# Group norms centred and spread by fp32r products, and FFN tiles begun earlier, in a decoder block on one core

## The chip, the core and the metric

The kernel runs on one core of one Trainium2 chip. A core has a matrix engine (PE, or TensorE), a vector engine (DVE), a scalar engine (ACT), a general engine (POOL, or GpSimd) and a queue engine (SP) that issues the transfers here. Each works through its own list of instructions in order, and waits on semaphores for the others. The metric is the device time of one execution in microseconds (us).

## The reference

Input is one sequence of 1024 tokens by 1024 channels, all float32. Cut to what matters:

```
h   = modulate(rmsnorm(x), shift1, scale1)
u, v, val, gate = split(h @ w_in + b_in)                     # 512 channels each
y_a = gelu(u) * (causal 128x128 mix of layernorm(gelu(v)) + b_s)
y   = val * sigmoid(gate)
y   = causal depthwise conv of y, width 31, + bias
y_b = silu(layernorm of y over groups of 64 channels)        # the group norm
x   = x + gate1 * (concat(rmsnorm(y_a), rmsnorm(y_b)) @ w_out)
h2  = modulate(rmsnorm(x), shift2, scale2)
x   = x + gate2 * ((silu(h2 @ w_g) * (h2 @ w_up)) @ w_ffn_out)   # FFN width 2816
out = modulate(rmsnorm(x), shift_f, scale_f)
```

## The kernel before

Channels lie on the 128 partitions, tokens along the free dimension, in two halves of 512 tokens. A tile of 128 channels by 512 tokens fits one PSUM bank.

**Products.** A float32 product is made of three fp32r products: each operand is split into a rounded part ("hi", an ACT copy) and the remainder ("lo", a subtraction on DVE or POOL), and PE adds hi x hi, lo x hi and hi x lo in one bank (`mm3`, L680, and `product`, L1068). Small products are left in true fp32, which PE runs as two records each in the trace. The FFN's products use a scheme of seven half-size products (m1 to m7) for eight; the sums of quadrants that this needs are DVE and POOL work (L1175 to L1180 for weights, L1200 to L1214 for activations).

**Stages.** For half 0 and half 1: first norm, projections (u, v, value/gate), spatial mixing, convolution, group norm, `w_out`, second norm. Then the FFN with 22 tiles of its width, its down projection in three rounds, and the last norm, which is written out in three pieces: half 0, then two of 256 tokens.

**Convolution and group norm.** Half 0's taps are shared by DVE and POOL, half 1's are all DVE's (L1006, two tiles at a time in a pair). `group_norm` (L1021) centres each tile by an fp32 product with the matrix `gcen` (L1026), squares on ACT, sums the squares by small products (L1033), takes root and reciprocal (L1036, L1037) and spreads the reciprocals back over channels and tokens: for half 0 by 16 fp32 products of 64 rows and 128 columns per pair (L1046), for half 1 by a block diagonal that DVE writes (`diagonal`, L614) and one fp32r product per tile (L1042).

**Work begun ahead.** For 20 of the 22 FFN tiles the two quadrant products that need only half 0 (m1 and m2, in 24 matmuls of 512 columns) are done by `ahead_quad` (L1082, traced under L1073 with the bank `ah`), and stored in HBM. 12 of them (`N_AHEAD`) are written in the program before half 1's convolution and output projection, 8 (`N_FILL`) behind the second norm of half 1. Each loads a weight tile of 512 KB, has its hi part made by ACT and its lo part (`wl_a`) by POOL, adds once on DVE (L1090) and stores 2 x 256 KB. The two other tiles (20 and 21) are done whole, tile 20 first.

**What sets the order.** The program's text gives only the dependences. `fix_order` (L499) runs a planner forward and backward over all instructions with a table of costs per kind of instruction, and the best of a few such plans becomes the fixed order of each engine. An instruction that the plan puts ahead of another on the same engine holds it up if its operands come late.

**Memory.** Tiles named `s` share four buffers (`tag="s"`, `bufs=4`); the FFN's own tiles take over the memory of the first stages and can be written only when these are through.

## Time and profile before

| | us |
|---|---|
| median of 3 runs | 967.76 (966.22 to 967.87) |
| the profiled execution | 967.97 |
| its span in the profile | 965.9 |
| PE busy / DVE busy / ACT busy / POOL busy | 950.5 / 871.7 / 474.0 / 408.6 |
| granted PE clock, mean | 0.995 |

The profiled execution agrees with the runs. PE's busy time is the union of its instructions, whose ends are modelled, so a PE that is always "busy" can still issue faster or slower: the spacing of its instructions tells which. A matmul's own duration in a row (0.39 us for 512 columns) overlaps the next one. Rows of instructions in order of time give the start, the duration, the engine, line and operation, the output, an arrow and the inputs, and how many alike follow each other; the chain of waits gives start, length and what ran.

### The profile page before, as it was taken

Reading aid. Unit: us, or ns where it says so; the run is one execution under the profiler, and the core shown is the slowest. Engines: PE = TensorE matmul, PEld = TensorE weight load, DVE = VectorE, ACT = ScalarE, POOL = GpSimd, SP = SyncE. Lnnn points to the kernel's source line nnn. Section 1 sums busy time; section 2 is a strip of 40 time slices with the busy share of each in tenths; the row PEclk is TensorE's granted clock in tenths of the full one; section 3 lists DMA queues with packets and bytes.
Section 4 is the critical chain, followed back from the end, with each engine's and each line's share of the span. In section 5 each row is a group of like instructions: output and inputs, shape, how many; then the busy total and the mean of one; then the engine's idle time right before and its main releaser. Section 6 shows DMA issues by size and latency. Waiting matters only on the chain.

```text
span 965.9 us, 12960 instructions
## 1 busy us (share of the span) xinstructions
PE 950.5 (98%) x4521; PEld 769.6 (80%) x4521; DVE 871.7 (90%) x1236; ACT 474.0 (49%) x756; POOL 408.6 (42%) x241
## 2 busy tenths in 40 slices
PE   8999999999999999999999999999999999999996
PEld 4887777778777778788888888888888888888885
DVE  6999999999999763999999999999879999969956
ACT  5787477643474753564333333333337437227426
POOL 0089988836453413665444444455433100000132
PEclk9999999999999999999999999999999999999998
DMA  9882542343485444844677678867657857415104
GB/s 353 323 310 91 176 152 69 113 174 131 137 282 188 158 136 146 271 173 147 215 245 239 230 237 261 268 211 257 211 177 264 266 172 258 162 33 159 61 1 174
DMA packets 70498, 184.24 MB, mean 191 GB/s; under 512 B 7841, under 2 KB 8353, under 8 KB 70434
## 3 DMA queue, kind: packets, MB, share of 16 engines
q1 hardware_dynamic: 70434, 183.43, 56.5%
q8 instruction: 35, 0.57, 0.2%
q14 instruction: 29, 0.24, 0.1%
...
## 4 chain that ended last, share of the span: by engine, by line
PE 79%; DVE 15%; ACT 2%; DMA 2%; issue 1%; SPq 0%; ACTq 0%; DVEq 0%
PE B L1073 30%; PE C L1073 18%; PE ah L1073 10%; DVE cv L1006 5%; PE A L1073 3%; PE v L682 2%; PE v L684 2%; PE po L682 2%; PE po L684 2%; PE v L683 2%; PE po L683 2%; PE p L684 1%; PE p L683 1%; PE p L682 1%; DVE ada L636 1%
## 5 line engine op out<-in xcount | busy, mean ns | idle before, releaser
L1073 PE MATMUL B<-h,w_f 128*128 128x512 f32 x816 | 189.6, 389 | 0.1
L1073 PEld LDWEIGHTS B<-h,w_f 128*128 128x128 f32 x816 | 153.0, 188 | 32.5 <-ACT x L1291 0.8
L1006 DVE SCALAR_TENSOR_TENSOR cv<-ypad,colt,cv 128x512 f32<-128x512 f32 x216 | 147.0, 744 | 0.2
L1073 PE MATMUL B<-fa,w_d 128*128 128x512 f32 x528 | 124.8, 389 | 0.1
L1073 PE MATMUL C<-h,w_f 128*128 128x512 f32 x528 | 123.4, 389 | 0.0
L1073 PEld LDWEIGHTS B<-fa,w_d 128*128 128x128 f32 x528 | 98.8, 188 | 21.4 <-DVE x L1433 0.7
L1073 PEld LDWEIGHTS C<-h,w_f 128*128 128x128 f32 x528 | 99.1, 188 | 20.6
L1073 PE MATMUL ah<-h,wh_a 128*128 128x512 f32 x320 | 102.4, 396 | 0.3 <-ACT h L699 0.3
L1359 POOL TENSOR_TENSOR sq_nf<-sq_nf,sq_nf 128x512 f32<-128x512 f32 (+1 forms) x15 | 18.0, 1202 | 170.2 <-ACT sq_nf L1353 170.0
L666 POOL TENSOR_TENSOR wl_a<-raw_a,wh_a 128x1024 fp32r<-128x1024 f32 x20 | 49.8, 2488 | 78.2 <-ACT wh_a L665 78.2
L1065 ACT ACTIVATE w_d<-raw_d 128x512 fp32r<-128x512 f32 (+1 forms) x72 | 42.0, 593 | 80.9 <-PE B L1073 32.6
L1065 ACT ACTIVATE w_f<-raw_f 128x512 fp32r<-128x512 f32 x68 | 42.5, 629 | 75.9 <-PE B L1073 41.5
L1316 POOL TENSOR_TENSOR x<-x,up 128x512 f32<-128x512 f32 x20 | 33.2, 1659 | 105.6 <-ACT x L1315 105.6
L1066 DVE TENSOR_TENSOR w_f<-raw_f,w_f 128x512 fp32r<-128x512 f32 x68 | 70.2, 1039 | 2.6 <-ACT w_f L1065 2.5
L1073 PEld LDWEIGHTS ah<-h,wh_a 128*128 128x128 f32 x320 | 60.0, 188 | 15.7 <-ACT h L699 1.4
L1073 PE MATMUL C<-fa,w_d 128*128 128x512 f32 (+1 forms) x291 | 63.9, 370 | 0.0
L1073 PE MATMUL ah<-h,wl_a 128*128 128x512 f32 x160 | 62.5, 390 | 0.0
L1073 PEld LDWEIGHTS C<-fa,w_d 128*128 128x128 f32 x291 | 51.0, 188 | 9.2
L1066 DVE TENSOR_TENSOR fa<-a,fa 128x512 fp32r<-128x512 f32 x77 | 52.4, 720 | 0.4 <-ACT fa L1065 0.4
L1433 DVE SCALAR_TENSOR_TENSOR x<-B,cond,x 128x512 f32<-128x512 f32 x48 | 35.6, 745 | 18.2 <-PE B L1073 18.0
L1066 DVE TENSOR_TENSOR w_d<-raw_d,w_d 128x512 fp32r<-128x512 f32 (+1 forms) x72 | 49.1, 691 | 1.1 <-ACT w_d L1065 1.1
L1065 ACT ACTIVATE fa<-a 128x512 fp32r<-128x512 f32 x77 | 46.1, 625 | 7.1 <-DMA a<-acts 4.0
...
## 6 DMA issues: line engine op xcount, KB each, us to landing
...
```

The costliest lines, as they stand in the source:

```text
L636: V.scalar_tensor_tensor(raw, raw, 1.0, cact, op0=ALU.mult, op1=ALU.mult, accum_out=cond[:, j:j + 1])
L666: lo_eng.tensor_tensor(lo[:, cut], raw[:, cut], hi[:, cut].bitcast(F32), op=ALU.subtract)
L682: PE.matmul(acc, shi, mhi, start=start, stop=False)
L683: PE.matmul(acc, slo, mhi, start=False, stop=False)
L684: PE.matmul(acc, shi, mlo, start=False, stop=stop)
L1006: V.scalar_tensor_tensor(accs[j], src, wc, accs[j], op0=ALU.mult, op1=ALU.add)
L1065: A.activation(dst[:, 0, :], src, AF.Copy)
L1066: lo_eng.tensor_tensor(dst[:, 1, :], src, dst[:, 0, :].bitcast(F32), op=ALU.subtract)
L1073: last_mm = PE.matmul(bank[:, cols], s, m[:, cols], start=first and p == 0 and i == 0, stop=p == n - 1 and i == 2, skip_group_check=True)
L1316: G.tensor_tensor(g0, g0, up0, op=ALU.mult)
L1359: G.tensor_tensor(run, run, t, op=ALU.add)
L1433: V.scalar_tensor_tensor(x_tile(k, part), bank[:, cols], ccol(GATE2, k), x_tile(k, part), op0=ALU.mult, op1=ALU.add)
```

## The change

- **Centring in half 1.** `group_norm` takes the convolution's sums directly. For a tile without POOL taps it makes a rounded part (ACT) and a remainder (DVE) and multiplies both by a rounded `gcen_r` in two fp32r products, where one fp32 product stood. Rounded parts, remainders and results use the tag `s`.
- **Spreads in half 0.** The 16 fp32 products per pair become the block diagonal and one fp32r product per tile, as in half 1. The diagonal, its rounded copy and the picking matrix lie in one more tile of the tag `raw`, which POOL clears.
- **Row sums** of the spatial weights (`rs`): two products of 64 output rows instead of two of 128, and four DVE steps of 128 rows for eight of 64.
- **Value/gate of half 1, tile 0** is written ahead of half 0's v projection.
- **Ahead tiles**: 14 before half 1's projection and 6 behind its norm, instead of 12 and 8.
- **The end**: ten idle matmuls into a spare bank between the last sums and the last norm's spread; the last shift on DVE; the last store in two halves.

```diff
-N_AHEAD = 12
-N_FILL = 8
+N_AHEAD = 14
+N_FILL = 6
+IDLE_LAST = (0, 0, 10)
...
         A.activation(late["picks"], raw, AF.Copy)
         G.memset(late["diag"].bitcast(F32), 0.0)
 
-    def diagonal(src):
-
-        diag, low = late["diag"], late["low"]
+    def diagonal(src, diag=None, low=None):
+
+        if diag is None:
+            diag, low = late["diag"], late["low"]
         A.activation(low, src, AF.Copy)
         for q in range(4):
             rows = slice(32 * q, 32 * q + 32)
...
     vsel = front.tile([P, 1], F32R, name="vsel")
     cstt = front.tile([P, P + 34], F32, name="cstt")
     gcen = cstt[:, 0:P]
+    gcen_r = front.tile([P, P], F32R, name="gcen_r")
 
     def gind(i):
         return cstt[:, P + 2 - 2 * i:P + 34 - 2 * i]
...
         V.tensor_tensor(vb[32:33], raw[32:33], vb[32:33].bitcast(F32), op=ALU.subtract)
         A.activation(vsel, col("sel_hl"), AF.Copy)
         nc.sync.dma_start(cstt, cst[:, 0:P + 34])
+        A.activation(gcen_r, gcen, AF.Copy)
 
     def spatial_bias():
-        for q in range(2):
-            rs = mm_bank(f"rs{q}")
-            PE.matmul(rs, ones.broadcast_to([P, P]), wt[:, 4 * q:4 * q + 4, :], start=True, stop=True)
-            for hh in range(4):
-                hd = 4 * q + hh
-                e, hp = hd % 2, hd // 2
-                rows = slice(e * 64, (e + 1) * 64)
-                V.scalar_tensor_tensor(bst[rows, hp, :], rs[rows, hh * P:(hh + 1) * P],
-                                       col("a_ln_b", hp)[rows], bst[rows, hp, :],
-                                       op0=ALU.mult, op1=ALU.add)
+        rs = mm_bank("rs")
+        heads = wt.rearrange("p (a e) t -> p e a t", e=2)
+        for e in range(2):
+            PE.matmul(rs[e * 64:(e + 1) * 64], ones.broadcast_to([P, 64]), heads[:, e], start=True, stop=True)
+        for hp in range(4):
+            V.scalar_tensor_tensor(bst[:, hp, :], rs[:, hp * P:(hp + 1) * P], col("a_ln_b", hp), bst[:, hp, :],
+                                   op0=ALU.mult, op1=ALU.add)
 
     idle = front.tile([P, H], BF16, tag="vn", name="idle", bufs=4)
     V.memset(idle, 0.0)
...
     def conv(half, jp, n_pool):
         if jp == 0:
-            conv_s[half] = [front.tile([P, H], F32, tag="s", name=f"s{half}_{j}", bufs=4)
+            conv_s[half] = [front.tile([P, H], F32, tag="s", name=f"s{half}_{j}", bufs=4) if n_pool else None
                             for j in range(4)]
         conv_pair(half, jp, n_pool, conv_s[half])
 
...
         for j in js:
             if n_pool:
                 V.tensor_tensor(s[j], s[j], accs[j], op=ALU.add)
-            else:
-                A.activation(s[j], accs[j], AF.Copy)
         with tc.high_priority():
-            group_norm(half, jp, js, s)
-
-    def group_norm(half, jp, js, s):
+            group_norm(half, jp, js, s, accs)
+
+    def group_norm(half, jp, js, s, accs):
         sqs = {}
         bank = {j: gn_bank(f"gn{half}_{j}") for j in js}
         b0, b1 = (bank[j] for j in js)
         for j in js:
-            PE.matmul(bank[j], gcen, s[j], start=True, stop=True)
+            if s[j] is not None:
+                PE.matmul(bank[j], gcen, s[j], start=True, stop=True)
+                continue
+            hi, lo = (front.tile([P, H], F32R, tag="s", name=f"s{n}{half}_{j}", bufs=4) for n in "hl")
+            A.activation(hi, accs[j], AF.Copy)
+            V.tensor_tensor(lo, accs[j], hi.bitcast(F32), op=ALU.subtract)
+            PE.matmul(bank[j], gcen_r, hi, start=True, stop=False)
+            PE.matmul(bank[j], gcen_r, lo, start=False, stop=True)
         for j in js:
+            if s[j] is None:
+                s[j] = front.tile([P, H], F32, tag="s", name=f"s{half}_{j}", bufs=4)
             sqs[j] = front.tile([P, H], F32, tag="ctmp", name=f"gsq{half}_{j}", bufs=2)
             A.activation(sqs[j], bank[j], AF.Square)
             A.activation(s[j], bank[j], AF.Copy)
...
         A.activation(sd, b0[:, 0:P], AF.Sqrt, bias=epst[:, 0:1])
         V.reciprocal(sd, sd)
         by_block = f"g{half}{jp}" not in DIAGONAL
-        both = sd if by_block else diagonal(sd)
+        picks = None
+        if by_block:
+            both = sb.tile([P, 2 * H], F32R, tag="raw", name=f"gd{half}{jp}", bufs=N_RAW)
+            diag, work = both[:, 0:H], both[:, H:]
+            G.memset(diag.bitcast(F32), 0.0)
+            picks = work[:, P:3 * P]
+            A.activation(picks.rearrange("p (a b) -> p a b", a=4), colt[:, _OFF["picks"]:_OFF["picks"] + 4].unsqueeze(2).broadcast_to([P, 4, 64]), AF.Copy)
+            both = diagonal(sd, diag, work[:, 0:P])
+        else:
+            picks, both = late["picks"], diagonal(sd)
         for i, (j, b) in enumerate(zip(js, (b1, b0))):
-            if not by_block:
-                PE.matmul(b, late["picks"][:, i * P:(i + 1) * P], both, start=True, stop=True)
-            for q in range(4):
-                for g in range(2):
-                    if by_block:
-                        PE.matmul(b[g * 64:(g + 1) * 64, q * P:(q + 1) * P],
-                                  col("sel_grp", 8 * i + 2 * q + g).broadcast_to([P, 64]), sd,
-                                  start=True, stop=True)
+            PE.matmul(b, picks[:, i * P:(i + 1) * P], both, start=True, stop=True)
             V.tensor_tensor(s[j], s[j], b, op=ALU.mult)
             A.activation(s[j], s[j], AF.Silu, bias=col("b_gn_b", j), scale=col("b_gn_g", j))
 
...
     u_proj(1)
     spatial_bias()
     background += [lambda i=i: ada_cols(SHIFT2 * 8 + i, pool=i < 12) for i in range(16)]
+    vg_proj(1, (0,))
     v_proj(0)
     conv(0, 0, N_POOL_TAPS[0])
     spatial(0, gn_bank)
...
     ya0 = a_out(0)
     spatial(1, gn_bank)
     yb0 = b_out(0)
-    vg_proj(1, (0, 1, 2))
+    vg_proj(1, (1, 2))
     w_out(0, ya0 + yb0)
     flush_background()
     finish_shift(SHIFT2, 0, 8)
...
     nc.sync.dma_start(eye, cst[:, P + 34 + 2 * P + 1:])
 
     pieces = [slice(0, H), slice(H, H + 256), slice(H + 256, S)]
-    sums, squares_in, norm_banks = {}, [0, 0, 0], {}
+    sums, squares_in, norm_banks, sum_ins = {}, [0, 0, 0], {}, {}
 
     def to_partitions(i, t):
 
         part = pieces[i]
         for q in range((part.stop - part.start) // P):
-            PE.matmul(norm_banks[i][:, q:q + 1], t[:, q * P:(q + 1) * P], ones,
-                      start=squares_in[i] == q == 0, stop=False, skip_group_check=True)
+            sum_ins[i] = PE.matmul(norm_banks[i][:, q:q + 1], t[:, q * P:(q + 1) * P], ones,
+                                   start=squares_in[i] == q == 0, stop=False, skip_group_check=True).ins
         squares_in[i] += 1
 
     def square(k, half, cols=None, late=False):
...
     def norm(i):
         bank, part = norm_banks[i], pieces[i]
+        for _ in range(IDLE_LAST[i]):
+            ins = PE.matmul(idle_bank[:, 0:2 * P], eye.bitcast(BF16)[:, 0:P], eye.bitcast(BF16), start=True, stop=True).ins
+            edges.append((ins.name, sum_ins[i].name))
         nq = (part.stop - part.start) // P
         rt = const.tile([P, nq], F32, name=f"rt_nf{i}")
         A.activation(rt, bank[:, 0:nq], AF.Sqrt, bias=epst, scale=1.0 / D)
...
             else:
                 V.scalar_tensor_tensor(t, x_tile(k, part), ccol(SCALEF, k), bank[:, 0:size],
                                        op0=ALU.mult, op1=ALU.mult)
-                A.activation(t, t, AF.Identity, bias=ccol(SHIFTF, k))
-            if (k + 1) % per_store == 0:
-                nc.sync.dma_start(out[(0, KD, KD + KD // 2)[i] + k // per_store], row)
+                if i == 2 and k == KD - 1:
+                    V.tensor_scalar(t, t, ccol(SHIFTF, k), None, op0=ALU.add)
+                else:
+                    A.activation(t, t, AF.Identity, bias=ccol(SHIFTF, k))
+            store = out[(0, KD, KD + KD // 2)[i] + k // per_store]
+            if i == 2 and k >= KD - per_store:
+                cut = slice(k % per_store * size, (k % per_store + 1) * size)
+                nc.sync.dma_start(store[:, cut], t)
+            elif (k + 1) % per_store == 0:
+                nc.sync.dma_start(store, row)
 
     DESTS = {1: (0, 0), 2: (0, 0), 5: (4, 1), 7: (4, 1), 6: (0, 1), 3: (0, 1), 4: (4, 0)}
     KEPT = {1: {5: 5, 3: 6}, 2: {5: 7, 3: 4}, 3: {5: 3, 3: 1}}
...
             rest(n, m)
         output(0, by_pool=BY_POOL)
         norm_banks[1], norm_banks[2] = gn_bank("ssq_nf1"), mm_bank("ssq_nf2")
+        idle_bank = gn_bank("idle_end")
         for i in (1, 2):
             part = pieces[i]
             cols = slice(part.start - H, part.stop - H)
```

How instructions move, in three places. The first is POOL around half 1's second norm, before and after (`wl_a14` is the remainder of ahead tile 14's weights; the `h2_` rows make half 1's quadrant sums, and begin behind the norm).

```order
L666 TENSOR_TENSOR wl_a14_3522<-raw_a14_3519,wh_a14_3521 128x1024
L666 TENSOR_TENSOR wl_a15_3559<-raw_a15_3556,wh_a15_3558 128x1024
L666 TENSOR_TENSOR wl_a16_3596<-raw_a16_3593,wh_a16_3595 128x1024
L1210 TENSOR_TENSOR h2_12_0_3742<-h2_22_0_3743,h2_12_0_3742 128x512
L666 TENSOR_TENSOR wl_a17_3633<-raw_a17_3630,wh_a17_3632 128x1024
L1214 TENSOR_TENSOR h2_21_0_3741<-h2_21_0_3741,h2_11_0_3740 128x512
L1210 TENSOR_TENSOR h2_12_1_3771<-h2_22_1_3772,h2_12_1_3771 128x512
L666 TENSOR_TENSOR wl_a18_3670<-raw_a18_3667,wh_a18_3669 128x1024
L1066 TENSOR_TENSOR h2_0_4_3763<-h2_21_0_3741,h2_0_4_3763 128x512
L666 TENSOR_TENSOR wl_a19_3707<-raw_a19_3704,wh_a19_3706 128x1024
```

After:

```order
L668 TENSOR_TENSOR wl_a16_3599<-raw_a16_3596,wh_a16_3598 128x1024
L668 TENSOR_TENSOR wl_a17_3636<-raw_a17_3633,wh_a17_3635 128x1024
L668 TENSOR_TENSOR wl_a18_3673<-raw_a18_3670,wh_a18_3672 128x1024
L1221 TENSOR_TENSOR h2_12_0_3745<-h2_22_0_3746,h2_12_0_3745 128x512
L668 TENSOR_TENSOR wl_a19_3710<-raw_a19_3707,wh_a19_3709 128x1024
L1225 TENSOR_TENSOR h2_21_0_3744<-h2_21_0_3744,h2_11_0_3743 128x512
L1221 TENSOR_TENSOR h2_12_1_3774<-h2_22_1_3775,h2_12_1_3774 128x512
L1076 TENSOR_TENSOR h2_0_4_3766<-h2_21_0_3744,h2_0_4_3766 128x512
```

Where three `wl_a` steps stood between POOL's first steps for `h2`, one stands now; the tiles behind them are two fewer.

The second place is PE at the first FFN tile (tile 20; `B`, `C`, `A` are its banks, `w_f20_2` the weights of m2), before:

```order
L1073 MATMUL B_20_3963<-h2_0_6_3756,w_f20_6_3947 128x512 x3
L1073 MATMUL B_20_3963<-h2_1_6_3785,w_f20_6_3947 128x512 x3
L1073 MATMUL B_20_3963<-h2_2_6_3814,w_f20_6_3947 128x512 x3
L1073 MATMUL B_20_3963<-h2_3_6_3843,w_f20_6_3947 128x512 x3
L1073 MATMUL A_20_4005<-h2_0_4_2292,w_f20_2_3950 128x512 x3
L1073 MATMUL A_20_4005<-h2_0_5_2299,w_f20_2_3950 128x512 x3
```

After:

```order
L1083 MATMUL B_20_3966<-h2_0_6_3759,w_f20_6_3950 128x512
L1083 MATMUL A_20_4008<-h2_0_4_2277,w_f20_2_3953 128x512
L1083 MATMUL B_20_3966<-h2_0_6_3759,w_f20_6_3950 128x512 x2
L1083 MATMUL B_20_3966<-h2_1_6_3788,w_f20_6_3950 128x512 x3
L1083 MATMUL B_20_3966<-h2_2_6_3817,w_f20_6_3950 128x512 x3
L1083 MATMUL B_20_3966<-h2_3_6_3846,w_f20_6_3950 128x512 x3
L1083 MATMUL A_20_4008<-h2_0_4_2277,w_f20_2_3953 128x512 x2
```

One matmul of A, with the weights `w_f20_2`, now stands ahead of eleven of B. The same happens behind m4 of this tile, with one matmul each of `C_20`, of the next tile's `B_0` and of its `C_0`.

The third place is DVE there: the steps that write these weights, before and after (`s3`, `raw` are sums of weights; `h2_3_7` is the last operand of m7).

```order
L1066 TENSOR_TENSOR w_f20_6_3947<-raw_f20_0_3933,w_f20_6_3947 128x512
L1066 TENSOR_TENSOR h2_2_6_3814<-h2_11_2_3798,h2_2_6_3814 128x512
L1066 TENSOR_TENSOR h2_3_6_3843<-h2_11_3_3827,h2_3_6_3843 128x512
L1066 TENSOR_TENSOR w_f20_2_3950<-raw_f20_0_3933,w_f20_2_3950 128x512
L1066 TENSOR_TENSOR w_f20_7_3953<-s3_f20_3937,w_f20_7_3953 128x512
L1175 TENSOR_TENSOR s3_f0_4038<-raw_f0_0_4034,raw_f0_1_4036 128x512
L1066 TENSOR_TENSOR h2_3_7_3846<-h2_12_3_3829,h2_3_7_3846 128x512
```

After:

```order
L1076 TENSOR_TENSOR w_f20_6_3950<-raw_f20_0_3936,w_f20_6_3950 128x512
L1076 TENSOR_TENSOR h2_3_6_3846<-h2_11_3_3830,h2_3_6_3846 128x512
L1076 TENSOR_TENSOR w_f20_2_3953<-raw_f20_0_3936,w_f20_2_3953 128x512
L1076 TENSOR_TENSOR w_f20_7_3956<-s3_f20_3940,w_f20_7_3956 128x512
L1076 TENSOR_TENSOR h2_2_7_3820<-h2_12_2_3803,h2_2_7_3820 128x512
L1186 TENSOR_TENSOR s3_f0_4041<-raw_f0_0_4037,raw_f0_1_4039 128x512
L1076 TENSOR_TENSOR h2_3_7_3849<-h2_12_3_3832,h2_3_7_3849 128x512
```

The order among them is the same but for `h2_2_7`: it stood further up before, and comes behind `w_f20_7` now.

9 lines of the change are left out of this document (4 added, 5 removed).

## Prediction

> **What bounds the kernel now.** I read the page's busy line first, then the busy times by stretch, then the chain of waits, and last the instructions in order of time at the places the change touches.
>
> ```profile
> PE 950.5 (98%) x4521; PEld 769.6 (80%) x4521; DVE 871.7 (90%) x1236; ACT 474.0 (49%) x756; POOL 408.6 (42%) x241
> core 0: us, PE busy (x) PEld busy (x) DVE busy (x) ACT busy (x) POOL busy (x), PEclk, DMA share, GB/s
> 202.00:260.00 58.00, 58.00 (x279) 47.28 (x278) 57.81 (x86) 23.02 (x30) 30.19 (x15) 1.00 0.42 140
> 260.00:320.00 60.00, 59.68 (x275) 46.92 (x275) 59.44 (x97) 35.13 (x54) 28.22 (x14) 1.00 0.64 214
> 320.00:345.00 25.00, 24.73 (x122) 18.09 (x120) 15.46 (x22) 20.46 (x30) 9.50 (x7) 1.00 0.46 156
> 345.00:390.00 45.00, 45.00 (x224) 36.20 (x223) 22.71 (x28) 16.33 (x21) 9.68 (x4) 1.00 0.40 136
> 390.00:444.00 54.00, 53.85 (x238) 44.15 (x236) 52.89 (x58) 31.48 (x52) 35.17 (x19) 1.00 0.59 202
> 393.00 28.29 PE ah L1073 x125
> ```
>
> PE is never idle for long: a fp32r product of 512 columns starts every 28.29 / 125 = 0.227 us. So PE work that goes shortens the time, unless something makes PE wait. The one engine near enough to do that is DVE: full from 202 to 320 and again from 390 to 444, and more than half idle between 345 and 390. ACT, POOL and DMA have room in every stretch. Today PE is covered by FFN tiles begun ahead, 12 of them before half 1's output projection and 8 behind it; those covers are what the change shifts.
>
> **The change part by part.**
>
> ```profile
> 107.79 1.72 PE rs L789 x4
> 144.45 1.90 PE gn L1046 x32
> 164.02 0.87 PE gn L1026 x2
> 322.08 1.13 PE gn L1026 x2
> 323.98 1.10 PE gn L1026 x2
> L620 DVE SCALAR_TENSOR_TENSOR late<-late,colt,gsd 32x128 fp32r<-32x128 f32 x8 | 3.7, 462 | 0.3 <-ACT late L617 0.2
> L1090 DVE TENSOR_TENSOR ahead<-ah,ahead 128x512 f32<-128x512 f32 x20 | 13.6, 680 | 2.6 <-PE ah L1073 2.5
> ```
>
> *Centring half 1.* Four fp32 products (two records each) cost 1.13 and 1.10 at the end of the convolution and, for the other pair, about the 0.87 of two records back to back: 3.97. Eight fp32r products take 8 x 0.227 = 1.82. Saves **2.2** (1.6 to 2.4).
>
> *Half 0's spreads.* 16 small fp32 products cost 1.90 per pair plus 0.20 in the next matmul's start; two products of 512 columns cost 0.45. Saves 1.65 per pair less little, **3.2** for both (2.8 to 3.4).
>
> *Row sums.* Two 64-column-wide products for four records of 0.43. At L1046's pace, 1.90 / 16 = 0.119 for 128 columns, two of 512 take 0.95: saves **0.8**. If the two don't overlap as L1046's do, nothing; 0 to 0.9.
>
> *What DVE pays for this.* Four remainders, at the 0.60 pace of its tensor_tensor, 2.4; eight writes of a diagonal, 0.35 each without interference, 2.8; four row-sum steps fewer, 1.4 (eight of 0.35 become four). DVE is 3.8 later at the end of half 1's convolution, where it is full. The fresh copies on ACT, the four of its rounding and the POOL memsets lie in engines half empty; uncovered, they'd be 0.2 to 0.6 each. Against the 3.8, PE comes to half 1's output projection 2 x 24 x 0.227 = 10.9 later for two more tiles and 6.2 earlier for the savings: +4.7. But rounded parts, remainders and results now share four buffers, so the second pair passes through them in turn, one or two steps of 0.6 longer. Before, PE starts on the second half of that projection with nothing to spare:
>
> ```profile
> 349.10 0.41 PE L682 MATMUL po<-y_b,wh_o 128*128 128x512 f32 x1
> 347.54 2.07 DVE L962 SCALAR_TENSOR_TENSOR yn_b<-s,colt,ssq_b 128x512 f32<-128x512 f32 x3 [1.66 <-PE ssq_b L733]
> ```
>
> PE takes up the first y_b at 349.10, while DVE writes the third input of the normalised y_b until 349.6. 4.7 against 3.8 + 1.2 is a wait of 0.3. The move of half 1's first value/gate product ahead of half 0's v likewise takes 48 matmuls from the cover at half 0's projection, leaving others there; I add 0.5. Together **+0.8** (0 to 2.5).
>
> *Six fills instead of eight.* This is the large term. Behind half 1's second norm (its product ends at 393.00) DVE must build the operands of the first FFN tiles while PE works on fills.
>
> ```profile
> 430.49 2.88 PE L1073 MATMUL B<-h,w_f 128*128 128x512 f32 x12
> 433.20 2.88 PE L1073 MATMUL C<-h,w_f 128*128 128x512 f32 x12
> 438.64 1.52 PE L1073 MATMUL A<-h,w_f 128*128 128x512 f32 x6
> 432.32 3.41 DVE w_f L1066 x2
> 437.42 1.70 DVE h L1066
> 445.06 0.68 DVE L1066 TENSOR_TENSOR w_f<-raw_f,w_f 128x512 fp32r<-128x512 f32 x1
> 399.07 2.92 POOL L666 TENSOR_TENSOR wl_a<-raw_a,wh_a 128x1024 fp32r<-128x1024 f32 x1 [1.75 <-ACT wh_a L665]
> 399.65 2.88 DVE L1066 TENSOR_TENSOR h<-h,h 128x512 fp32r<-128x512 f32 x1
> 410.15 2.85 POOL L666 TENSOR_TENSOR wl_a<-raw_a,wh_a 128x1024 fp32r<-128x1024 f32 x1
> 410.67 0.68 DVE L1090 TENSOR_TENSOR ahead<-ah,ahead 128x512 f32<-128x512 f32 x1
> 411.27 2.28 DVE L1211 TENSOR_TENSOR h<-h,h 128x512 f32<-128x512 f32 x1
> ```
>
> Before, the first of the two w_f at 432.32 (operand of A) is done at 434.0 and used at 438.64: 4.6 to spare. In the new order 118 matmuls, not 165, stand between the norm and the first FFN product, so PE is there 26.8 after the norm, not 37.5; and the new order sets the first matmul of A behind 25 more, at 32.5, and the second tile's first C behind 74 more, at 43.6. DVE in the old trace has A's operand at 434.0 - 393.0 = 41.0 and that C's (the w_f at 445.06) at 52.7. It is relieved of two L1090, 1.2; of one L1180 that comes later, 0.6; and of two of POOL's wl_a. These hold up a DVE instruction that runs against them: 2.88 and 2.28 instead of 0.68, so 2.2 and 1.6, while the L1090 beside one takes 0.68. Both kinds occur; I take 1.8 for each, 3.6. Relief 5.4, so the C's operand is there at 47.3, and PE waits 47.3 - 43.6 = **3.7** in all, most of it at A (41.0 - 5.4 - 32.5 = 3.1; the late L1180 is no relief there, but an h step that now comes behind A's operand is). Bounds: all of POOL's 2.9 given back, relief 1.8 + 5.8 = 7.6, wait 1.5; POOL's steps fall where they cost DVE nothing, relief 1.8, wait 7.3. I stay at 3.7: the two rows of held-up instructions are nearest to it. The transfers and stores of two tiles go to a stretch with DMA at 0.40 to 0.46, and cost nothing there.
>
> What POOL's two wl_a do at their new place, beside the convolution, is a question of its own:
>
> ```profile
> 227.16 7.33 DVE L1006 SCALAR_TENSOR_TENSOR cv<-ypad,colt,cv 128x512 f32<-128x512 f32 x11
> 228.07 2.40 POOL L666 TENSOR_TENSOR wl_o<-raw_o,wh_o 128x1024 fp32r<-128x1024 f32 x1
> 230.42 1.30 POOL L724 TENSOR_TENSOR sq_n<-sq_n,sq_n 128x512 f32<-128x512 f32 x1
> ```
>
> Eleven taps take 7.33, 0.66 each, though POOL runs for 3.7 of them: here nothing is held up. [...]
>
> *The end.*
>
> ```profile
> 954.15 0.53 PEld L1377 LDWEIGHTS ssq_nf<-eye,rt_nf 128*128 128x128 f32 x4
> 957.54 0.93 PEld L1377 LDWEIGHTS ssq_nf<-eye,rt_nf 128*128 128x128 f32 x4 [1.57 <-DVE rt_nf L1375]
> 944.11 0.89 PE ssq_nf L1377 x8
> 957.54 1.24 PE ssq_nf L1377 x4
> 960.23 2.10 ACT of L1401 x5
> 960.32 2.77 SPq L1403 DMA_DIRECT2D out<-of  x4
> ```
>
> The last norm's spread takes 1.24 for four records where 944.11 has 0.11 each, 0.44, and its weight loads 0.93 against 0.53: PE's clock fell in the wait ahead of it. Ten idle matmuls of 256 columns, 0.227 / 2 = 0.11 each, put 1.1 of work into that wait: I take 0.6 of the 0.8 that can be had. The last shift is added by DVE while ACT does the one before it, and the last store is cut in two, so that the last 128 KB wait for one tile: 0.4, about one ACT step (2.10 / 5). **1.0**, between -0.3 (idle matmuls in the way, an extra issue) and 1.3.
>
> [...]
>
> *Sum.* -2.2 - 3.2 - 0.8 + 0.8 + 3.7 - 1.0 = **-2.7**. The profiled execution took 967.97, 0.2 over the median 967.76, so I count from the median: **965.1**.
>
> **The rivals.**
> (A) No new wait at the FFN's start: the 4.6 to spare and a relief of 7.6 cover it. Then 965.1 - 3.7 = 961.4. For it speaks that DVE's steps there can also change places. Against it: even with that relief 41.0 - 7.6 - 32.5 = 0.9 would be left at the first A.
> (B) The other side: DVE gets no relief at the FFN's start, because its steps there only meet other POOL steps. The wait at the C is then 52.7 - 43.6 = 9.1, 5.4 more than I take: 970.5. It decides from a wait of 8.3 on, where it passes the other terms' 6.4 by 0.2%. For it: POOL is busy for 35.17 of 54.00 there, and fewer steps may only draw the rest together. Against it: the 1.2 of two L1090 goes in any case, and 399.65 and 411.27 met just these steps.
> (C) y_b of half 1 comes late: 2.5 more at half 1's projection, through the shared buffers: 967.6, no measurable change. PE's start at 349.10 without room speaks for it, the wl_o and L1090 steps that DVE can put off there, against.
> (D) The two moved wl_a hold up half 1's taps as they hold up other DVE steps, 2 x 2.40 = 4.8, which PE sees at the projection: 969.9. The taps at 227.16 speak against it. [...]
>
> **How the numbers follow.** 0.2% (1.9 us) is about what a measurement of this kernel can tell from no change. Forecast 0.58, own range 963.0 to 967.2 (wait 1.6 to 5.8); A 0.14; B 0.11; C 0.11; D 0.06. Faster means under 965.8: 0.46 of the forecast, A, and 0.04 of C: 0.64. Same, 965.8 to 969.7: the other 0.12 of the forecast, 0.07 of C, 0.02 of D: 0.21. Slower: B and the rest of D, 0.15. The range 961.0 to 969.2 leaves out B, most of D and a little of A, under 2 in 10.
>
> **What would show it.** After: two products of 512 columns where L1046's group of 32 was, for each pair of half 0; about 0.45 for a centring; rs at 0.95; the last L1377 near 0.5 of its length; behind the last fill one or two idle times of PE, ended by DVE's w_f, of 2 to 5 in sum, the longest ahead of the first A. The prediction is wrong if PE has no gap there (A), if the gaps exceed 8 (B), or if PE waits over 2 for y_b before half 1's projection (C); and if taps of half 1 run slower than 0.66 beside POOL (D).

## The result and the profile after

| | before | after |
|---|---|---|
| median | 967.61 (966.22 to 968.66) | 973.47 (969.44 to 978.36, 10 runs) |
| ratio, 95% interval | | 1.0065 (1.0050 to 1.0081) |
| profiled execution / its span | 967.97 / 965.9 | 969.44 / 967.6 |

The change makes the kernel 0.65% slower; 965.1 was predicted. Its executions also scatter over three times as wide. The profiled one is the shortest of its ten, 4.0 below their median; a second profiled execution of the same kernel (976.15, the first experiment) shows what the longer ones do.

The page's busy line of the kernel after, and the busy times by stretch, in the stretches that the prediction shows of before:

```profile
PE 949.3 (98%) x4470; PEld 765.9 (79%) x4471; DVE 873.6 (90%) x1245; ACT 473.1 (49%) x760; POOL 405.9 (42%) x243
...
202.00:260.00 58.00, 57.94 (x290) 46.72 (x289) 57.87 (x87) 21.79 (x30) 32.42 (x17) 1.00 0.44 151
260.00:320.00 60.00, 59.51 (x268) 48.47 (x268) 59.00 (x93) 31.88 (x48) 29.81 (x14) 1.00 0.69 223
320.00:345.00 25.00, 24.95 (x131) 18.44 (x130) 20.18 (x29) 20.89 (x33) 8.85 (x6) 1.00 0.42 142
345.00:390.00 45.00, 44.35 (x202) 35.99 (x201) 24.13 (x31) 19.53 (x26) 9.03 (x5) 1.00 0.42 146
390.00:444.00 54.00, 53.36 (x258) 42.34 (x257) 48.97 (x55) 28.47 (x49) 32.72 (x19) 1.00 0.52 180
```

The picture by share of busy time is almost the one of before. That is the first lesson of this case: PE is "busy" 98% in both, and what is lost lies in many small waits. The instructions in order of time at the changed places (PE's row sums, spreads, one centring of half 1 and the longest waits up to the FFN; DVE's diagonal of half 0's first pair):

```profile
107.56 1.08 PE L794 MATMUL rs<-wt,ones 128*64 128x512 f32 x4
157.48 0.62 PE L1058 MATMUL gn<-gd 128*128 128x512 f32 x2
185.01 1.16 PE L739 MATMUL ssq_a<-rt_a,sel_tok 128*128 128x128 f32 x8 [0.90 <-DVE rt_a L733]
187.17 0.50 PE L1058 MATMUL gn<-gd 128*128 128x512 f32 x1 [0.54 <-DVE gd L622]
329.68 0.47 PE L1031 MATMUL gn<-sh,gcen_r 128*128 128x512 f32 x1
329.98 0.39 PE L1032 MATMUL gn<-sl,gcen_r 128*128 128x512 f32 x1
357.18 0.50 PE L684 MATMUL po<-y_b,wh_o 128*128 128x512 f32 x1 [0.65 <-ACT y_b L965]
151.72 5.31 DVE L622 SCALAR_TENSOR_TENSOR gd<-gd,colt,gsd 32x128 fp32r<-32x128 f32 x4
```

The products shrank as forecast, or nearly: summed over PE's instructions up to the first FFN product (each from its start to the next start), the spreads of half 0 take 1.02 instead of 3.94, all centring 4.55 instead of 6.00, the row sums 1.01 instead of 1.66. That is 5.0 less. But in the same sum the value/gate products of both halves, with the idle matmuls among them, grew from 95.58 to 98.04 (1.9 of it in half 1), and both halves' output projections from 87.63 to 88.77, and the FFN starts at 427.62 instead of 430.49, only 2.9 earlier. In the second profiled execution it starts at 431.90, later than before.

From there the busy times by stretch show how many matmuls PE gets done (the number in the first brackets), before and after:

```profile
425.00:450.00 25.00, 24.87 (x110) 20.26 (x110) 24.30 (x30) 14.28 (x25) 13.62 (x8) 1.00 0.36 114
450.00:600.00 150.00, 150.00 (x664) 124.20 (x662) 148.40 (x190) 47.22 (x78) 70.57 (x43) 1.00 0.72 238
600.00:800.00 200.00, 200.00 (x883) 165.31 (x882) 182.83 (x248) 78.53 (x132) 74.27 (x45) 1.00 0.70 227
```

```profile
425.00:450.00 25.00, 24.54 (x106) 19.10 (x105) 25.00 (x29) 15.42 (x27) 14.39 (x9) 1.00 0.28 98
450.00:600.00 150.00, 149.89 (x662) 123.90 (x661) 149.66 (x189) 49.06 (x80) 70.65 (x44) 1.00 0.70 232
600.00:800.00 200.00, 198.23 (x866) 161.67 (x865) 180.67 (x246) 76.85 (x130) 74.61 (x45) 1.00 0.69 230
```

4 + 2 + 17 = 23 matmuls fewer at 0.227 are 5.2 us, and 17 of the 23 are missing not at the FFN's opening, where the prediction had put the loss, but after 600. Two places in order of time, one at the opening and one at the turn to the down projection:

```profile
436.39 1.43 PE L1083 MATMUL A<-h,w_f 128*128 128x512 f32 x5 [0.22 <-DVE w_f L1076]
736.81 3.02 PE L1083 MATMUL B<-h,w_f 128*128 128x512 f32 x12 [1.04 <-ACT x L1302]
```

The end, in order of time, gained: the last spread's weight loads take 0.52 (0.93 before), and from the last FFN product to the end of the span pass 11.18 instead of 11.76.

```profile
958.19 1.25 PE L1384 MATMUL idle_end<-eye 128*128 128x256 bf16 x10
959.82 0.52 PEld L1391 LDWEIGHTS ssq_nf<-eye,rt_nf 128*128 128x128 f32 x4 [0.66 <-DVE rt_nf L1389]
```

So for this execution: -2.9 (front) + 5.2 (FFN) - 0.6 (end) = +1.7, against 969.44 - 967.97 = 1.5 measured. The other 4 us of the median lie in the front and the FFN of the longer executions.

### The profile page after: what moved, and what is told of

Its sections match the earlier page's. It is cut to its first block, busy times and chain, and to the rows that moved or that the text cites. A ratio compares the mean times of both kernels' runs of the same rounds, so it can differ in the third digit from the quotient of the medians.

```text
span 967.6 us, 12887 instructions
## 1 busy us (share of the span) xinstructions
PE 949.3 (98%) x4470; PEld 765.9 (79%) x4471; DVE 873.6 (90%) x1245; ACT 473.1 (49%) x760; POOL 405.9 (42%) x243
## 4 chain that ended last, share of the span: by engine, by line
PE 81%; DVE 10%; DMA 4%; ACT 3%; issue 2%; SPq 0%; POOL 0%; DVEq 0%; ACTq 0%; POOLq 0%
PE B L1083 27%; PE C L1083 17%; PE ah L1083 10%; PE A L1083 3%; PE po L684 3%; PE po L685 3%; PE po L686 3%; PE pu L686 2%; PE pu L684 2%; PE pu L685 2%; DVE w_f L1076 1%; PE v L686 1%; PE v L685 1%; PE v L684 1%; PE p L684 1%
## 5 line engine op out<-in xcount | busy, mean ns | idle before, releaser
L1083 PE MATMUL B<-h,w_f 128*128 128x512 f32 x816 | 192.7, 391 | 1.9 <-ACT x L1302 1.3
L1330 POOL TENSOR_TENSOR x<-x,u 128x512 f32<-128x512 f32 x22 | 37.3, 1698 | 70.0 <-DVE u L1329 39.4
```

The costliest lines, as they stand in the source:

```text
L1083: last_mm = PE.matmul(bank[:, cols], s, m[:, cols], start=first and p == 0 and i == 0, stop=p == n - 1 and i == 2, skip_group_check=True)
L1330: G.tensor_tensor(g1, g1, u2, op=ALU.mult)
```

## The experiments

Each was timed in five rounds beside the kernel before, whose median was 967.08 to 967.43 in the five groups of runs. "Lost" is the time from the start of a 512-column matmul to PE's next start, above 0.227, summed over a stretch; a lower granted clock behind a wait (0.51 over 750 to 755 us of e12) is part of it.

| run | what | median | ratio (95%) |
|---|---|---|---|
| e1 | the changed kernel again | 973.32 | 1.0060 (1.0038 to 1.0081) |
| e2 | before, 14 ahead and 6 fills | 972.36 | 1.0053 (1.0033 to 1.0073) |
| e3 | after, 12 ahead and 8 fills | 976.63 | 1.0079 (1.0057 to 1.0102) |
| e4 | after, old end | 974.42 | 1.0061 (1.0040 to 1.0082) |
| e5 | after, old spreads of half 0 | 974.47 | 1.0070 (1.0053 to 1.0087) |
| e6 | after, value/gate of half 1 at its old place | 990.87 | 1.0246 (1.0226 to 1.0266) |
| e7 | after, old centring of half 1 | 973.32 | 1.0058 (1.0045 to 1.0072) |
| e8 | before, new row sums and new end | 968.54 | 1.0011 (1.0003 to 1.0020) |
| e9 | e4 with the FFN order of e2 | 975.16 | 1.0072 (1.0057 to 1.0087) |
| e10 | e2 with the FFN order of e4 | 974.00 | 1.0069 (1.0053 to 1.0084) |
| e11 | before, new end | 966.56 | 0.9996 (0.9986 to 1.0006) |
| e12 | before, new spreads of half 0 | 982.28 | 1.0142 (1.0122 to 1.0163) |
| e13 | e12, diagonal laid mostly by ACT | 975.62 | 1.0091 (1.0076 to 1.0106) |
| e14 | after, diagonal laid mostly by ACT | 975.86 | 1.0079 (1.0059 to 1.0099) |
| e15 | e3, diagonal laid mostly by ACT | 972.49 | 1.0056 (1.0039 to 1.0074) |
| e16 | before, new centring of half 1 | 975.36 | 1.0077 (1.0061 to 1.0092) |
| e17 | before in another order (DVE's delay) | 970.08 | 1.0029 (1.0018 to 1.0039) |
| e18 | before in another order (ACT's delay) | 971.33 | 1.0041 (1.0029 to 1.0054) |

Three theories stood at first. S: the FFN is paced by DVE, whatever the order. T: the order that the planner writes for the changed kernel is a bad one, above all near 735 us. D: the diagonals of half 0 make DVE late beside POOL (this is not the prediction's rival D).

**e1: the changed kernel once more**, for a second profile.

> The changed kernel itself, once more, for its spread and another profile. Its ten executions lay between 969.44 and 978.36, where the kernel before had 966.22 to 968.66. Theory S (the FFN now begins about 3 us earlier, and DVE, not PE, sets its pace): loss spread over the FFN's 300 us in small waits of PE for DVE, much the same in each execution. Theory T (the newly planned order leaves the turn from the FFN's first product to its second, near 735 us, with too little time between storing and loading the activations): median 971 to 976 again, and the waits of PE that exceed those of before sit near 730 to 760 us and differ from execution to execution by several us.

973.32; the profiled execution took 976.15 and started its FFN at 431.90. Both executions run the same instructions in the same order, and part at about 187 us. Rows of DVE and POOL in order of time, first of the execution of 969.44, then of this one:

```profile
187.15 0.55 DVE L922 TENSOR_SCALAR vn<-vn,mv,sd 128x512 f32<-128x512 f32 x1
187.32 2.64 POOL L668 TENSOR_TENSOR wl_o<-raw_o,wh_o 128x1024 fp32r<-128x1024 f32 x1 [3.50 <-ACT wh_o L667]
```

```profile
187.93 2.73 DVE L922 TENSOR_SCALAR vn<-vn,mv,sd 128x512 f32<-128x512 f32 x1
187.99 2.40 POOL L668 TENSOR_TENSOR wl_o<-raw_o,wh_o 128x1024 fp32r<-128x1024 f32 x1 [3.39 <-ACT wh_o L667]
```

In the one DVE is 0.17 ahead and its instruction takes 0.55; in the other the two start 0.06 apart and DVE's takes 2.73. An accumulation of `ada` meets POOL in the same way at 209.5 (3.44 instead of 1.22). These two put 4.4 us on DVE, and the FFN starts 4.3 later: between these two executions, the difference up to the FFN is who comes first. That the whole scatter has this cause isn't shown. In the second pair of rows DVE's instruction starts 0.06 ahead of POOL's and yet ends at 190.66, 0.27 behind POOL's end.

**e2 and e3: the split of the ahead tiles alone, and all but it.**

```diff
 e2, in the kernel before:        e3, in the changed kernel:
-N_AHEAD = 12                     -N_AHEAD = 14
-N_FILL = 8                       -N_FILL = 6
+N_AHEAD = 14                     +N_AHEAD = 12
+N_FILL = 6                       +N_FILL = 8
```

> The kernel before with 14 tiles ahead of half 1's projection and 6 behind its norm, and nothing else. DVE then has 10.9 us less cover behind the norm and is relieved by about 5.4. Theory S: 3 to 6 us over before, 970 to 974. Theory T: the order is planned anew, so anything from 964 to 975, and the difference to before lies near 730 to 760 us. The forecast's own term says 967.6 + 3.7 = 971.

> The changed kernel with the old 12 tiles ahead and 8 behind. Theory S: the late DVE has its cover back, the savings stay: 961 to 963. Theory T: the front saves 6 us up to the FFN's start, and what is left of it at the end depends on the new order: 962 to 972.

e2 took 972.36, 5.0 more than before. It loses 4.9 at 420 to 440, in one wait, and the lower clock behind it (eleven matmuls take 4.37, twelve took 2.88 at 430.49 of before; the granted clock is 0.93 over 425 to 450), for the kind of operand that the prediction named, though for another product (in order of time):

```profile
437.44 4.37 PE L1073 MATMUL B<-h,w_f 128*128 128x512 f32 x11 [3.37 <-DVE w_f L1066]
```

e3 took 976.63: with 12 and 8 the changed kernel is slower still, and above what either theory gave. It loses only 3.8 in the FFN, but 11.6 at 320 to 360, where the changed kernel loses 2.7. By stretch, e3 and the changed kernel at 320 to 362:

```profile
320.00:362.00 42.00, 37.39 (x153) 26.68 (x152) 31.61 (x46) 25.64 (x39) 9.04 (x7) 0.88 0.28 94
```

```profile
320.00:362.00 42.00, 41.30 (x207) 31.25 (x206) 31.23 (x46) 29.08 (x46) 11.43 (x8) 1.00 0.39 133
```

The granted clock (the third number from the right) is 0.88 in e3, so part of the 11.6 is the lower clock behind the waits: behind one of 1.57 for `y_b` at 354 the products start 0.43 apart, not 0.227. So the two extra tiles take some 5 us from the FFN's cover and give more than that to half 1's group norm, whose longer chain would otherwise stop PE. The split is a loss by itself and a need of the rest.

**e4, e8 and e11: the end and the row sums.**

```diff
 e4, in the changed kernel (e11 is the reverse of it, in the kernel before):
-IDLE_LAST = (0, 0, 10)
+IDLE_LAST = (0, 0, 0)
...
-                if i == 2 and k == KD - 1:
-                    V.tensor_scalar(t, t, ccol(SHIFTF, k), None, op0=ALU.add)
-                else:
-                    A.activation(t, t, AF.Identity, bias=ccol(SHIFTF, k))
+                A.activation(t, t, AF.Identity, bias=ccol(SHIFTF, k))
...
-            if i == 2 and k >= KD - per_store:
+            if False:
```

> The changed kernel without its end: no idle matmuls, last shift on ACT, last store in one. From the last products on it should be 1.0 us slower (0.3 to 1.3). Theory S: total 974.5, 1 over the changed kernel. Theory T: since the whole order is planned anew, the total may differ from the changed kernel's by more than 3 us either way, by waits near 735 us, although nothing before the end was edited.

> The kernel before with only the row sums and the end of the change. Neither gives DVE more work (four steps fewer for the row sums, one step more at the end), so by theory D their savings stay: 0.65 from the row sums, 1.0 at the end, 965.7 to 966.2 with the small scatter of before. Theory T: the order is planned anew and total and scatter may go anywhere, 964 to 975.

> The kernel before with the new end alone: ten idle matmuls, the last shift on VectorE, the last stores in pieces. Up to the last block of the output the plan is that of the kernel before. The prediction's term for the end is 1.0: 966.4. The changed kernel's trace has 0.58 of it: 966.8. If the idle matmuls or the extra stores cost what they save: 967.4 or more.

Without the new end the changed kernel takes 974.42, 0.95 more; the new end alone takes 0.66 off the kernel before (966.56 against 967.22). Neither is clear of the noise: the ratios of e4 and e1 are 1.0061 and 1.0060, and that of e11 has 1 inside its interval. Up to the end e11's order is that of before, and its trace loses 1.45 in the FFN where before loses 1.3. From the last FFN product to the end of the span pass 11.2 in it, as in the changed kernel, and 11.76 before. With the row sums added (e8) the median is 968.54, 2.0 above e11: they save 0.65 of matmuls, and in the newly planned order e8 loses 2.8 more than before ahead of the FFN (among others 0.65 at half 1's `y_b`). So theory D's expectation for e8, 965.7 to 966.2, failed: DVE has no more work there, and the savings are gone all the same.

**e5, e6 and e7: one part taken back from the changed kernel.**

```diff
 e5: the 16 fp32 products per pair of half 0 again
...
-            PE.matmul(b, picks[:, i * P:(i + 1) * P], both, start=True, stop=True)
+            for q in range(4):
+                for g in range(2):
+                    PE.matmul(b[g * 64:(g + 1) * 64, q * P:(q + 1) * P],
+                              col("sel_grp", 8 * i + 2 * q + g).broadcast_to([P, 64]), sd, start=True, stop=True)
 e6: value/gate of half 1 all behind b_out(0)
-    vg_proj(1, (0,))
...
-    vg_proj(1, (1, 2))
+    vg_proj(1, (0, 1, 2))
 e7: half 1 centred by the fp32 product of the copied sums
-            conv_s[half] = [front.tile(...) if n_pool else None
+            conv_s[half] = [front.tile(...)
...
+            else:
+                A.activation(s[j], accs[j], AF.Copy)
```

> The changed kernel with half 0's spreads by 16 small fp32 products per pair again, nothing else. Theory D: the diagonals of half 0 are what makes DVE late there: its four steps for the first pair took 1.30 each beside POOL's taps instead of 0.35, and PE, which has no such wait before, then waits 2.5 to 5 behind value/gate products and 1 to 3 in half 0's projection. Then PE pays 2.9 for the old spreads and gets 3 to 6 back, the total falls to 970 to 973 and scatters less, with no wait over 0.3 between 140 and 220 us. Theory T (any new order does as it likes): waits of 2 us and more stay in that stretch.

> The changed kernel with half 1's first value/gate product back behind half 0's mixing, so 48 matmuls more lie at half 0's projection. If the lost cover there is the cause of PE's waits at 180 to 215 us, they go, and the total falls by 2 to 4, to 969.5 to 971.5. Under theory D (diagonals late on DVE) the waits move but stay, and the total is within 1.5 of 973.4.

> The changed kernel with half 1's centring by fp32 products again. PE pays 1.5 to 2.2 more for them, DVE is relieved of four remainders (2.4) and the second pair of the passage through shared buffers, so half 1's normalised y_b comes 3 to 5 earlier. If that y_b is what holds PE at 357 us (0.65 there), the two nearly cancel: 972 to 975. If centring was a gain as forecast: 975.5.

e5 (974.47) and e7 (973.32) can't be told from the changed kernel: neither the spreads nor the centring, as they stand in it, are worth anything that these runs can tell. e5 has no wait of PE over 0.6 from 128 to 271 us. Up to the FFN it loses 16.1, the changed kernel 18.4 and 22.6 in its two profiled executions: what the new spreads save in matmuls, 2.9, goes there into waits. In the FFN e5 loses 9.1, the changed kernel 6.5 and 8.9. e6 (990.87, where less time was expected) was the surprise: the value/gate products, which the prediction had booked as a small cost, are worth 17 us. Without them ahead of half 0's v projection, PE stands before DVE's results all through half 0 (in order of time):

```profile
153.60 1.97 PE L948 MATMUL pm<-wt,vn 128*64 128x128 f32 x32 [0.83 <-DVE s L1059]
173.04 2.54 PE L1026 MATMUL gn<-s,cstt 128*128 128x512 f32 x4 [2.19 <-DVE sd L919]
```

**e9 and e10: the two FFN orders exchanged**, to tell S from T. e4 and e2 have the same 4051 instructions in the FFN.

```diff
+    for turn in FFN_ORDER.values():
+        turn = [nc.cur_bb.bb.instructions[ffn_from + int(k)].name for k in turn.split()]
+        edges.extend(zip(turn[1:], turn))
     fix_order(tc, edges, ("mid", "front"), "ffn", 3)
```

> The program is that of the run with the old end (974.42). Its front is planned as there, instruction for instruction; in the FFN every engine is made to follow the order that the planner gave to the kernel before with 14 tiles ahead and 6 fills, whose FFN consists of the same 4051 instructions. Theory T, that the FFN loses its time because the new plan puts other steps in its rows: TensorE's matmuls of 128x512 lose 1 us or less between 600 and 800 us, where the old-end run loses 4.8, and the time falls to 970 to 971.5 if the FFN's opening keeps its 0.6; if the opening takes the 4.9 that the 14-and-6 kernel shows there, it stays near 974. Theory S, that the FFN is paced by VectorE whatever the order, since the new front hands over earlier with fewer steps done: 4 us or more are lost between 600 and 800 us again, and the time stays at 973 to 976.

> The mirror: the program is the kernel before with 14 tiles ahead and 6 fills (972.36), its front planned as there; in the FFN every engine follows the order that the planner gave to the changed kernel with the old end. Theory T: TensorE loses 4 us or more between 600 and 800 us, where the 14-and-6 kernel loses 0.8, and the opening's 4.9 shrink to 1 or less if the opening is a matter of the order too; 972 to 976. Theory S: 1 us or less between 600 and 800 us, and 972 or below.

Matmuls by stretch, 425 to 450 and 600 to 800, of e2, e10, e4 and e9 in turn (before: 110 and 883):

```profile
425.00:450.00 25.00, 21.63 (x88) 17.17 (x87) 24.89 (x28) 14.96 (x26) 14.54 (x9) 0.93 0.32 98
...
600.00:800.00 200.00, 200.00 (x882) 165.04 (x882) 184.66 (x248) 78.25 (x132) 73.88 (x45) 1.00 0.69 230
```

```profile
425.00:450.00 25.00, 24.57 (x106) 19.10 (x105) 25.00 (x29) 14.08 (x25) 13.60 (x8) 1.00 0.26 95
...
600.00:800.00 200.00, 196.60 (x861) 160.94 (x860) 178.73 (x245) 75.24 (x128) 74.09 (x45) 1.00 0.70 230
```

```profile
425.00:450.00 25.00, 24.60 (x106) 19.15 (x105) 25.00 (x29) 15.00 (x27) 13.59 (x8) 1.00 0.28 95
...
600.00:800.00 200.00, 197.66 (x863) 161.05 (x862) 180.89 (x246) 75.78 (x129) 73.78 (x45) 1.00 0.69 228
```

```profile
425.00:450.00 25.00, 21.64 (x89) 17.33 (x88) 25.00 (x27) 13.26 (x25) 16.57 (x10) 0.93 0.26 81
...
600.00:800.00 200.00, 198.87 (x876) 163.84 (x876) 182.97 (x247) 75.93 (x128) 76.26 (x46) 1.00 0.69 232
```

The order moved with the exchange, and with it the place of the loss: the order of e2 loses 22 and 21 matmuls at the opening and 1 and 7 later, that of e4 loses 4 and 4 at the opening and 20 and 22 later. With those of 450 to 600, 1 to 3 each, the sums are 24, 28, 26 and 31 matmuls, 5.4 to 7.0 us, and the times didn't improve (974.00 after 972.36, 975.16 after 974.42). e10 came out as T expected on record, e9 nearly. S as recorded expected 4 us or more lost between 600 and 800 in e9 and 1 or less in e10, and failed both times (1.8 and 5.1). T says where PE waits. It doesn't say how much: all four lose 6.8 to 8.8 in the FFN, where before loses 1.3. That this is what two tiles fewer behind half 1's norm take away, in any order, is the nearest reading, but it isn't the whole: e12 and e17 below have all 8 fills and lose 6.6 and 4.2 between 600 and 800. e17 has no instruction changed, and gets as few matmuls done there as the changed kernel:

```profile
600.00:800.00 200.00, 197.38 (x866) 161.72 (x865) 182.27 (x244) 77.17 (x130) 77.31 (x45) 1.00 0.68 224
```

DVE is busy for 145 to 150 of the 150 us from 450 to 600 in all of these, and for 148 in the kernel before.

**e12 and e16: the spreads alone and the centring alone**, in the kernel before, and **e13 to e15: the diagonal with one DVE product** for four (ACT lays the blocks).

```diff
 e13, e14, e15, for half 0:
         A.activation(low, src, AF.Copy)
-        for q in range(4):
-            rows = slice(32 * q, 32 * q + 32)
-            V.scalar_tensor_tensor(diag[rows, q * P:(q + 1) * P], low[rows].bitcast(F32), col("low_rows")[rows], src[rows],
-                                   op0=ALU.mult, op1=ALU.add)
+        V.scalar_tensor_tensor(low, low.bitcast(F32), col("low_rows"), src, op0=ALU.mult, op1=ALU.add)
+        for q in range(4):
+            rows = slice(32 * q, 32 * q + 32)
+            A.activation(diag[rows, q * P:(q + 1) * P], low[rows].bitcast(F32), AF.Copy)
```

> The kernel before with half 0's spreads taken from the change alone (diagonal and one product for each channel tile instead of sixteen fp32 ones). The plan of the FFN is that of the kernel before, step for step; only the front differs. The prediction's term is 3.2 less: 964.2. Theory D, that the first pair's four diagonal products run at 1.30 instead of 0.35 beside GpSimd's taps and leave VectorE late behind them, so that the value and projection matmuls wait: half or more of the 3 us is lost again, 966 to 968.5. If the spreads are what makes the changed kernel slow: 970 or more.

> The run with the spreads alone (982.28), but a pair's high and low rows are made by one product of 128x128 on VectorE, and ScalarE lays the four blocks of the diagonal: VectorE loses 6 of its 8 products in half 0, 4 to 8 us beside GpSimd. Theory D (VectorE is full in 100 to 215 us, and what is added there delays TensorE): the waits of 1.8 to 2.6 us at 172, 190 and 195 us shrink and the half clock behind them goes; 968 to 975. If the new order of the front alone costs the 15 us: 979 or more. The prediction's term, 3.2 less than before, would be 964.

> The same edit in the changed kernel (973.47): in half 0 one product on VectorE and four blocks on ScalarE. Theory D: the FFN starts 2 to 4 us earlier than in the changed kernel's runs (427.6 and 431.9), and the time is 970 to 972; the FFN keeps the 6 to 9 us that TensorE loses there, since VectorE is full in it and the two tiles more ahead have taken cover from its opening. If the order alone matters: 973 to 978.

> The same edit with 12 tiles ahead and 8 fills (976.63 without it). Theory D: TensorE's 11.6 us at 320 to 360 us for half 1's y_b shrink by as much as VectorE is ahead at 215 us, some 4, and with the FFN's small loss (4) the time falls to 968 to 973. If that wait has a cause of its own in half 1, it stays at 975 to 978.

> The kernel before with half 1's centring by two fp32r products of the rounded part and the remainder alone. The prediction's term is 2.2 less: 965.0. The changed kernel's trace has 1.45 less of these matmuls, and its run without them is no slower (973.32 against 973.4): if VectorE's four subtractions in half 1 or the new order take it back, 967 to 970.

e12 took 982.28: the spreads alone cost 15 us, with the FFN in the very order of before. Its busy times by stretch at 100 to 215, behind those of before:

```profile
100.00:215.00 115.00, 115.00 (x679) 89.96 (x678) 114.27 (x165) 68.64 (x103) 88.66 (x46) 1.00 0.43 140
```

```profile
100.00:215.00 115.00, 106.95 (x580) 82.47 (x579) 114.37 (x157) 63.99 (x98) 87.40 (x47) 0.97 0.40 133
```

DVE, the third pair of numbers, was full there before (114.27 of 115). With the diagonals added, it gets through 157 instructions there instead of 165, and the FFN starts at 441.36, 10.9 late. The rest of e12's loss lies in the FFN, 7.7 where before loses 1.3 in the same order; why, stays open. The diagonals themselves cost DVE 3.2 and 3.5 a pair in e12, 5.31 in the first pair of the changed kernel, where eight at 0.35 had been forecast. Behind the first pair's the four `vn` steps of half 1 take 9.2; they met POOL in the kernel before too, and took 6.7. Rows of e12's DVE and POOL in order of time, and then PE's waits:

```profile
171.89 3.94 DVE L922 TENSOR_SCALAR vn<-vn,mv,sd 128x512 f32<-128x512 f32 x2
176.35 5.24 DVE L922 TENSOR_SCALAR vn<-vn,mv,sd 128x512 f32<-128x512 f32 x2
172.97 2.58 POOL L667 TENSOR_TENSOR wl_vg<-raw_vg,wh_vg 128x1024 fp32r<-128x1024 f32 x1
176.39 2.40 POOL L667 TENSOR_TENSOR wl_vg<-raw_vg,wh_vg 128x1024 fp32r<-128x1024 f32 x1 [0.85 <-ACT wh_vg L666]
...
172.12 1.10 PE L1027 MATMUL gn<-s,cstt 128*128 128x512 f32 x2 [1.84 <-DVE s L1016]
195.40 1.09 PE L948 MATMUL pm<-wt,vn 128*64 128x128 f32 x16 [2.41 <-DVE mx L952]
750.90 5.49 PE L1076 MATMUL B<-h,w_f 128*128 128x512 f32 x12 [2.64 <-ACT x L1294]
```

And each of these three waits costs a second time, in PE's clock. Twelve matmuls at 750.90 take 5.49, where twelve of the same kind took 3.02 in the changed kernel at 736.81. By stretch the granted clock is:

```profile
170.00:180.00 10.00, 8.16 (x32) 5.16 (x31) 10.00 (x9) 3.71 (x6) 8.49 (x4) 0.83 0.44 157
195.00:200.00 5.00, 3.73 (x22) 3.00 (x23) 5.00 (x4) 2.28 (x3) 5.00 (x4) 0.72 0.67 236
750.00:755.00 5.00, 4.10 (x10) 3.23 (x11) 4.30 (x7) 3.96 (x8) 0.00 (x0) 0.51 0.86 277
```

With three of four products taken from DVE, e12 falls from 982.28 to 975.62 (e13) and e3 from 976.63 to 972.49 (e15): as theory D has it, by 6.7 and 4.1 us. Both are also newly planned orders, which alone can be worth up to 4 (e17 and e18 below), so the 4.1 isn't proof. In the changed kernel itself (e14) the time rose, from 973.4 to 975.86, as was expected if the order alone matters: its profiled execution, the longest of its six (978.68), starts the FFN at 430.69 and loses 12.7 behind that. So D is very likely a cause, and not the whole of it.

e16, the centring alone, took 975.36, 8.3 more and above either expectation, for 4 fp32 products turned into 8 fp32r ones, four subtractions and a new order. A loss of 4.2 (0.1 in the kernel before) lies at 200 to 220 us, ahead of the centring, which begins at 275. DVE in order of time, then POOL, then PE's wait:

```profile
199.76 2.28 DVE L651 TENSOR_TENSOR cond<-cond,colt 128x8 f32<-128x8 f32 x1
202.62 1.77 DVE L652 SCALAR_TENSOR_TENSOR cond<-cond,colt 128x8 f32<-128x8 f32 x1
199.62 4.75 POOL L666 TENSOR_TENSOR wl_o<-raw_o,wh_o 128x1024 fp32r<-128x1024 f32 x2 [4.45 <-PE p L683]
207.99 1.61 PE L737 MATMUL ssq_b<-rt_b,sel_tok 128*128 128x128 f32 x8 [2.25 <-DVE rt_b L731]
```

Two instructions on 128x8 elements hold DVE for 4 us, beside two steps of POOL; before, in another order, the same two took 1.05 and 0.15.

**e17 and e18: the kernel before, no instruction changed, in two other orders**, which its planner writes when one of its assumed signal delays is 0.016 us longer.

```diff
 e17:
-SIGNAL = {"PE": 0.043, "DVE": 0.024, "Activation": 0.024, "Pool": 0.068, "SP": 0.05}
+SIGNAL = {"PE": 0.043, "DVE": 0.04, "Activation": 0.024, "Pool": 0.068, "SP": 0.05}
 e18:
+SIGNAL = {"PE": 0.043, "DVE": 0.024, "Activation": 0.04, "Pool": 0.068, "SP": 0.05}
```

> The kernel before, instruction for instruction, with the planner's assumed delay from VectorE to the others 0.040 instead of 0.024: 274 rows of VectorE's order differ (the centring alone: 140, the spreads alone: 112) and 69 of TensorE's (70 and 128). If the order alone is what the single parts paid for: 971 or more, with TensorE losing 4 us or more in new places before the FFN or in it. If the order is worth little and the parts themselves cost it: 966 to 969.

> The same with the assumed delay from ScalarE 0.040 instead of 0.024: 289 rows of VectorE's order differ and 175 of TensorE's. Order alone: 971 or more. Parts themselves: 966 to 969.

970.08 and 971.33: the order alone costs 2.7 and 3.9. The second is what was expected if the order alone matters, the first lies between the two expectations. The kernel before stands in an order that happens to suit the chip. A change that makes the planner write another can give 3 to 4 us away before it has done anything (two such orders were tried).

No kernel here beats the one before by more than its interval; e11 is level with it.

## Why the prediction was wrong, by its steps

By the sum the FFN had to start 5.4 earlier, at 425.1, and to cost 3.7 more. It started at 427.62 and 431.90 in the two profiled executions, 2.5 and 6.8 later than that, and cost 5.2 and 7.6 more. So the larger miss lies ahead of the FFN, where the first four terms stand.

- **Centring, -2.2.** The sum above has 1.45, but it books on the next matmul what an fp32 product delays it by (behind the one at 267.37 of before the next matmul takes 0.64 from start to start, not 0.227). With that, half 1's four old products take 3.9 without idle time and the eight new ones 1.9: 2.0 saved, nearly the forecast. As time it is worth nothing that can be told (e7) or costs 8.3 (e16).
- **Half 0's spreads, -3.2.** The matmuls gave 2.9, booked the same way. As time they are worth nothing that can be told in the changed kernel (e5) and cost 15 alone (e12).
- **Row sums, -0.8.** 0.65 of matmuls; with the end, 2.0 more time than the end alone (e8 against e11).
- **"What DVE pays for this", +0.8. This is the step that failed.** It counted DVE's additions at their undisturbed durations, and felt them at one place only, the end of half 1's convolution. The stretches it shows begin at 202 us; half 0's diagonals lie at 150 and 186, in a stretch where DVE was busy for 114.27 of 115. What the runs show in its place: DVE has no room there, its additions count in full and more (5.31 for four diagonal products forecast at 1.4), and PE pays unless other work is put in front of it (15 us in e12, with the spreads alone). The +0.5 for value/gate had the wrong sign and size: that move is the cover, 17.5 us of it in the changed kernel (e6). The same term calls DVE more than half idle from 345 to 390; its row has 22.71 of 45.00, which is half busy.
- **A term that was missing: the new order.** Every duration of an untouched instruction was carried over. Two orders of untouched instructions cost 2.7 and 3.9 (e17, e18), and e16 shows one way: which DVE instructions lie beside POOL's is drawn anew.
- **Six fills for eight, +3.7.** The mechanism and nearly the size were right where the split stands alone: it measures 5.0 (e2), with the longest wait for `w_f` behind the last fill. That PE would wait 2 to 5 there in the changed kernel was wrong; its order loses 4 matmuls there and 17 after 600. e9 and e10 move the loss from one place to the other with the order; but since e17 loses 17 after 600 with all 8 fills, how much of it is the two tiles' stays open.
- **The end, -1.0.** 0.58 in the trace; 0.66 and 0.95 by the medians, within the noise. Behind the idle matmuls (1.25 us) and a wait of 0.66 the spread takes 0.52 for its weight loads, at a granted clock of 1.00; before, behind a wait of 1.57, it took 0.93 at 0.50.
- **Rivals.** B (9.1 at the FFN's start) is out: 4.9 in e2. C (half 1's `y_b` late) was underrated: with the waits of the group norm ahead of it and the lower clock behind them (0.88 over 320 to 362), 11.6 is lost there in e3, and the wait is only 0.65 in the changed kernel because of the two extra tiles. D (taps held up by POOL) did not come: none of the 124 taps of half 1 takes over 0.82. Held up beside POOL, at the rows shown, are the diagonals (5.31 for four), `vn` (2.73) and `cond` (2.28). In the front, the prediction looked at the taps alone.

What stays open: how the 8.3 of the centring alone splits between the new order and its four subtractions (about half of it is lost ahead of them); in the same way, how the 15 of the spreads alone splits between DVE's work and the new order of the front; and what the value/gate move does in the kernel before, where it wasn't run alone. No single part was run with the order held.
